# Two transformer blocks with grouped experts on one core: the uneven expert pairs in four column strips of 32

## The chip, the cores and the metric

The program runs on one core of a Trainium2 chip. The metric is the device time of one execution in microseconds (us), taken as the median of several runs; lower is better. All inputs and weights are fp32 and lie in the chip's main memory at the start. The engines are named as the profile names them: PE (TensorE, matmul), PEld (its weight loads), DVE (VectorE), ACT (ScalarE), POOL (GpSimd) and SP (SyncE, which issues the DMAs).

## What is computed

The reference chains two blocks of two layers each over 256 tokens of width 1024. The first block has feed-forward halves, an attention mixer and a gated mixer; the second has a retention and attention mixer in its first layer, a stick-breaking mixer in its second, and after each of the two a mixture of 16 experts. Only that mixture matters here:

```python
def grouped_moe(h, router_w, router_b, w_gate, w_up, w_down):
    t = h.reshape(B_ * S, D)
    scores = jax.nn.sigmoid((t @ router_w).astype(jnp.float32))
    ...            # best of four groups of experts, then the two best experts in it
    y = jnp.zeros((t.shape[0], D), jnp.float32)
    for e in range(N_EXPERTS):
        he = jax.nn.silu(t @ w_gate[e]) * (t @ w_up[e])
        y = y + combine[:, e:e + 1] * (he @ w_down[e]).astype(jnp.float32)
    return y.reshape(B_, S, D).astype(h.dtype)
```

D is 1024, an expert is 512 wide, and each token goes to two experts of one group. Which tokens go where depends on the data, so the length of each expert's list is known only while the program runs.

## The kernel before

The program is one long sequence of stages on one core. PE does nearly everything; the weights stream in through SP's queue. The last stage of each of the second block's layers is the function `moe`, called twice: once with `l=0` and once with `l=1`. I call them the first and the second expert stage.

An expert stage works on eight pairs of experts, e and e + 8, which are in different groups, so that no token is in both lists. A pair has 128 slots, and the slots lie on the columns of the stationary operand: `x[:, k, o:o+m]` holds 128 values of the width for m slots. The slots are split between the two experts at run time, in units of 32: `gi` holds 2 (64 and 64 slots), 3 (96 and 32) or 1 (32 and 96) for each pair. A pair split 64 to 64 is called even below, the others uneven. What doesn't fit comes later in a loop of extra rounds.

`products` multiplies the slots with the weights: for each k it issues a row of products whose output strips lie side by side on the 128 output partitions, `p[o:o + m, :]`, 512 columns of weights each, and the table `SEG` says which strips (first slot, how many, which expert). I call the products of one k a step. As the split is known only at run time, there are three versions of each row of products (`arm(2)`, `arm(3)`, `arm(1)`) behind two branches (L1852, L1855), and PE's sequencer jumps to the one that the pair needs. A pair has three products of eight steps: `pg` (gate), `pu` (up) and `pd` (down, in two parts of four steps, each behind branches of its own), 24 steps in all. Between `pu` and `pd` PE gathers the next pair's tokens (`ga`) and transposes (`tr`); after `pd` it brings the results back to the tokens (`py`).

The experts' weights come as pieces of 1 MB, twelve to a pair, through a ring of 20 buffers (`RING`), filled ahead while the stage before is still running. Once the ring is full, `pieces` loads in halves of 512 KB, and each load (`piece`, L1618) waits on SP until PE has finished with that half of the buffer's old contents. SP issues these in one fixed order.

Each fp32 product appears in the trace as two records (a MATMUL of PE for each, with a LDWEIGHTS of PEld), so a step of two products is four records and a step of three is six.

Of the kernel before, what the change touches and what calls it, by code (L numbers as in the profile page):

```python
# [17 lines left out]
KD = 8  # L18
T = 256
# [13 lines left out]
def _const_arrays():  # L33
    f = np.float32
    c = {}
    p = np.arange(128)
# [4 lines left out]
    t = np.arange(T)  # L41
# [27 lines left out]
    for h in range(4):  # L69
        lg = np.log(1.0 - 2.0 ** (-5.0 - h))  # L70
        for mt in range(2):
            m = (mt * 128 + p)[:, None]
# [6 lines left out]
    # the heads' means of squares from column tile ct to rows 2 ct, 2 ct + 1, and from those rows back  # L79
# [24 lines left out]
def pipeline(units, width, bg=None, rate=1):  # L104
    """advance generators side by side, oldest first; a new one joins each round while fewer than width run.
    bg: generators worked through in the background, rate steps a round"""
    units, act, bg, due = list(units), [], list(bg or []), 0
    def back(n):
        while bg and n > 0:
            if next(bg[0], bg) is bg:  # L110
                bg.pop(0)
            else:
                n -= 1
    while units or act:
        if units and len(act) < width:
            act.append(units.pop(0))
        for g in list(act):
            if next(g, act) is act:
                act.remove(g)
        due += rate  # L120
        back(int(due))
        due -= int(due)
    back(1 << 30)


def build(tc, I, out, dump=None, upto=99):
    nc = tc.nc
    coff, ctot = _const_layout()
    with ExitStack() as ctx:
# [11 lines left out]
        # the two buffers of a stage's intermediate result, in floats  # L141
# [3 lines left out]
        def big(name, shape, dt=F32):  # L145
            """the next of the 16 KB buffers for weights as they come: two for the whole program and some of the
            stage's own"""
# [6 lines left out]
        def big2(name, shape, dt=F32R):  # L154
            """the next of the 16 KB buffers for split weights"""
            return wk.tile(shape, dt, name=name, tag="whl", bufs=NW)

        def pair_of(shape, names):
            """the two 12 KB buffers that hold a stage's intermediate result in two parts"""
# [73 lines left out]
        late = []  # L233

        def spawn(gen):
            """a generator's first step now, the others a tick each: between them other products run"""
# [24 lines left out]
        def mod_out(p, b0, nt, bias, dsts):  # L261
            """p: a quarter of the columns on each quarter of the partitions, vector v on its row v"""
# [13 lines left out]
        def mod_pe(w, b0, nt, si, bias, dst, dst2=None):  # L276
            """a step for each 128 rows of w: its load, and what follows it"""
# [13 lines left out]
        def mod_first(w, b0, bias, dst, dst2, bufs, ahead_=None):  # L291
            """8 column tiles, the rows two tiles at a time, all loads at once"""
# [17 lines left out]
        def mod_dve(w, b0, nt, si, bias, dst):  # L310
            """as mod_pe"""
# [61 lines left out]
        def filler(work):  # L373
            """steps of the modulation vectors, as many as are due for the work done"""
# [13 lines left out]
        def gains(name, m, j, g, neg=False):  # L388
            """gains (1 + scale) g, or with the other sign, and shifts of chunks j + 1 and j of the modulation m"""
# [11 lines left out]
        def rsqrt(r, p, lnexp):  # L401
            """r = 1/sqrt(p + eps)"""
# [7 lines left out]
        def wsplit(src, shape):  # L410
            """the weights' upper 12 bits and the rest, exactly"""
# [10 lines left out]
        def halves(src, pin=lambda ins: ins, eng=V):  # L422
            """256 columns of weights [128, KD, 256] or [128, KD, s, t, d], as wsplit, in two steps: a function that
            gives the two parts of column tile t"""
# [27 lines left out]
        class Sum:  # L452
            """the sum of squares of the tiles given, and from it 1/sqrt(mean + eps) on every partition"""
# [14 lines left out]
            def neg_rstd(self, stat, r, pin=False):  # L468
                """-1/sqrt(mean + eps): by exp and ln, and a Newton step"""
# [20 lines left out]
        class Stream:  # L490
            """h = X G rstd + S for the matrix products: X G in two parts, S as columns 256, 257; rstd and the
            products with S come in after them (fin)"""

            def __init__(self, X, gs, tag="h", pool=None, sums=None, neg=False, u=None):
                """neg: gains and rstd of the other sign; u: X rstd, then rstd is in the products"""
# [3 lines left out]
            def shift(self):  # L499
                """S into its columns"""  # L500
# [5 lines left out]
            def start(self, late=False):  # L506
                """late: without S"""
# [16 lines left out]
            def rs(self):  # L524
                """asked for after the first products"""
# [5 lines left out]
            def product(self, name, wh, wl):  # L531
                """wh, wl: [128, KD, 128]"""
# [9 lines left out]
            def fin_act(self, dst, p, func, ps=None):  # L542
                """ps: the product with S"""
# [6 lines left out]
        def ffn(w13, w2, streams, gates, parts, gp, first=None):  # L550
            """x += half gate * (silu(h wa) * (h wb)) w2, in parts of the hidden width; first: the weights of the first
            two hidden tiles, loaded, and the steps by which the shifts come, which their products don't wait for"""
# [19 lines left out]
            def up(j0, np_, g, j):  # L572
                """g[j] = silu(h wa) (h wb)"""
# [18 lines left out]
            def early(g, j, wh, wl):  # L592
                """up, the products with the shifts after the others"""
# [37 lines left out]
            def down(j0, np_, g, d):  # L631
                """x += gate * g w2 of this part"""
# [28 lines left out]
                # the first column tile's last hidden tile comes after the second column tile's others  # L661
# [25 lines left out]
        def load13(w13, j):  # L687
            """the columns of hidden tiles j and j + 1, of both halves"""
# [6 lines left out]
        def ahead(steps, begin):  # L695
            """steps of two parts each, the first part (weights) a step ahead of the second"""
# [15 lines left out]
        def chain(items):  # L712
            """items: (raw, columns in raw, [products], consume): the weights are split an item ahead of their products;
            consume(column tile of the item, product, psum); the first step is the first weights, the others a product"""
# [15 lines left out]
            # the first product's follow-up, which asks for rstd, comes after the second product  # L730
# [24 lines left out]
        def dense(w, c0, ncols, product, consume, block=512):  # L755
            """chain items of w's columns c0..; consume(column tile, psum)"""
# [28 lines left out]
        def need(*keys):  # L785
            """the steps put off that make these"""
# [14 lines left out]
        def out_proj(raw, o, gate, early, rest, n):  # L801
            """x += gate * o w, a column tile a step; the first step is the first weights, in the next 2 n the tiles of
            `rest` are left out, to follow when they are ready; after[0](column tile): what goes on from there"""
# [54 lines left out]
        def transposes(srcs):  # L858
            """the transposes of srcs, each [128, 128], four to a bank"""
# [10 lines left out]
        def finish(d2, y=None):  # L870
            """two column tiles of the result"""
# [9 lines left out]
        # =================== first block ===================  # L881
# [5 lines left out]
        def load_x(X, src):  # L887
            """X and X rstd"""
# [16 lines left out]
        with ExitStack() as c1:  # L905
# [7 lines left out]
            # scales first, then the shifts  # L913
# [47 lines left out]
        with ExitStack() as c1:  # L961
# [7 lines left out]
            # rstd of the queries' heads: columns 4 t + 2 tt + s  # L969
# [3 lines left out]
            # a tile of queries is heads t and t + 4, so that its halves meet the two heads of the keys  # L973
# [11 lines left out]
            def head_norm(x, n, g):  # L985
                """x [128, n] in place"""
# [7 lines left out]
            def rope(x, perm, cos, sin):  # L994
                """x [128, 256] in place"""
# [25 lines left out]
            def q_in(t, p):  # L1021
                """without rstd, which comes in with the scores"""
# [15 lines left out]
            def p_in(g, p):  # L1038
                """pools: windows of 2, 4, 8, 16 tokens by doubling"""
# [34 lines left out]
            def attend(t, tt, s):  # L1074
                """head t + 4 s, queries tt"""
# [92 lines left out]
        with ExitStack() as c1:  # L1168
# [13 lines left out]
            # the second block's relative bias, its ends repeated, to DRAM  # L1182
# [72 lines left out]
        # =================== second block ===================  # L1255
# [795 lines left out]
```

## Time and profile before

| what | value |
|---|---|
| runs (us) | 2150.61, 2151.38, 2154.91 |
| median (us) | 2151.38 |
| span of the profiled execution (us) | 2151.2 |
| PE busy | 2062.4 us, 96% |
| DVE busy | 1289.6 us, 60% |
| ACT busy | 734.3 us, 34% |
| mean DMA rate over the span | 249 GB/s |
| instructions in the trace | 34307 |

The profiled execution's own time is known as its span, from the first to the last instruction; it lies 0.2 us under the median of the runs. Busy PE means that a matmul was in the array, not that the array was at its full rate: two products that run side by side on different strips count once. So the share of 96% says only that PE is hardly ever without work, and what a stretch could lose must be read from how its products follow one another.

### The profile page before, as it was taken

How to read it: one execution, taken by the hardware profiler on the slowest of the kernel's cores; microseconds unless marked ns; L12 is line 12 of the kernel's file. 1: busy time of each engine (PE TensorE's matmuls, PEld its weight loads, DVE VectorE, ACT ScalarE, POOL GpSimd, SP SyncE). 2: the span in 40 equal slices, each digit the busy share in tenths (PEclk: the TensorE clock that was granted, in tenths of full speed). 3: DMA queues.
4: the chain of work that ended last, by engine and by line, in shares of the span. 5: the costliest groups of instructions: out<-in, count | busy, mean ns of one | idle time of the engine just before them, and what ended most of it. 6: DMA issues, size and time to landing. Idle time of an engine off the chain costs nothing. (4 is left out here: it accounts for less than half of the span.)

```text
span 2151.2 us, 34307 instructions
## 1 busy us (share of the span) xinstructions
PE 2062.4 (96%) x14152; PEld 1609.6 (75%) x14152; DVE 1289.6 (60%) x2188; ACT 734.3 (34%) x1075; POOL 67.6 (3%) x60
## 2 busy tenths in 40 slices
PE   6999999999999999999999999989998998999998
PEld 5889798986799999999999998744445984222343
DVE  5367687577697888877988678532225763111122
ACT  4222132254454454356544454410003762000001
POOL 0000000020100010000100100000001000000000
PEclk8999999999999999999999999999999998999999
DMA  8678688542487686955779364799996458666793
GB/s 299 217 272 313 238 319 285 179 137 79 151 306 250 213 307 241 337 173 196 261 249 328 125 222 141 258 336 386 385 383 236 138 210 307 228 232 228 267 386 119
DMA packets 307684, 534.57 MB, mean 249 GB/s; under 512 B 12717, under 2 KB 167713, under 8 KB 294177
## 3 DMA queue, kind: packets, MB, share of 16 engines
q1 hardware_dynamic: 306960, 531.55, 70.9%
q8 instruction: 150, 2.46, 0.5%
q14 instruction: 46, 0.37, 0.0%
q10 hardware_dynamic: 528, 0.20, 0.0%
HBM read 530.64 MB, written 1.06 MB: 247 GB/s over the span
## 5 line engine op out<-in xcount | busy, mean ns | idle before, releaser
L448 PE MATMUL pa<-hh,whl 128*128 128x258 f32 (+1 forms) x880 | 252.3, 287 | 3.5 <-ACT hh L516 3.5
L449 PE MATMUL pa<-hl,whl 128*128 128x258 f32 (+1 forms) x880 | 249.3, 283 | 2.7 <-DVE hl L517 2.7
L448 PE MATMUL pb<-hh,whl 128*128 128x258 f32 (+1 forms) x880 | 249.0, 283 | 0.7 <-ACT s L564 0.7
L450 PE MATMUL pa<-hh,whl 128*128 128x258 f32 (+1 forms) x880 | 249.0, 283 | 0.0
L449 PE MATMUL pb<-hl,whl 128*128 128x258 f32 (+1 forms) x880 | 248.6, 283 | 0.0
L450 PE MATMUL pb<-hh,whl 128*128 128x258 f32 (+1 forms) x880 | 248.5, 282 | 0.0
L418 ACT ACTIVATE whl<-w13r 128x2048 fp32r<-128x2048 f32 x88 | 168.6, 1916 | 191.7 <-PE pb L450 96.0
L324 DVE SCALAR_TENSOR_TENSOR macc<-modw,cst,macc 128x1024 f32<-128x1024 f32 (+1 forms) x182 | 220.1, 1236 | 15.8 <-DMA modw<-in_w_mod_dram 14.4
L419 DVE TENSOR_TENSOR whl<-w13r,whl 128x2048 fp32r<-128x2048 f32 x88 | 201.7, 2292 | 38.0 <-ACT whl L418 37.9
L450 PE MATMUL py<-gh,whl 128*128 128x256 f32 (+1 forms) x704 | 217.0, 309 | 2.5 <-DVE whl L419 2.5
L448 PE MATMUL py<-gh,whl 128*128 128x256 f32 (+1 forms) x704 | 218.8, 311 | 0.1
L449 PE MATMUL py<-gl,whl 128*128 128x256 f32 (+1 forms) x704 | 216.8, 308 | 0.0
L448 PE MATMUL lin<-hh,whl 128*128 128x258 f32 x640 | 189.2, 296 | 5.4 <-ACT hh L516 5.4
L449 PE MATMUL lin<-hl,whl 128*128 128x258 f32 x640 | 182.5, 286 | 2.8 <-DVE hl L517 2.8
L450 PE MATMUL lin<-hh,whl 128*128 128x258 f32 x640 | 181.9, 285 | 0.0
L448 PEld LDWEIGHTS pa<-hh,whl 128*128 128x128 f32 x880 | 166.4, 189 | 11.5 <-ACT hh L516 3.7
L449 PEld LDWEIGHTS pa<-hl,whl 128*128 128x128 f32 x880 | 167.5, 190 | 3.4 <-DVE hl L517 3.1
L448 PEld LDWEIGHTS pb<-hh,whl 128*128 128x128 f32 x880 | 166.6, 189 | 1.8 <-ACT s L564 0.9
L450 PEld LDWEIGHTS pa<-hh,whl 128*128 128x128 f32 x880 | 167.1, 190 | 0.4 <-issue 0.4
L450 PEld LDWEIGHTS pb<-hh,whl 128*128 128x128 f32 x880 | 166.5, 189 | 0.4 <-issue 0.4
L449 PEld LDWEIGHTS pb<-hl,whl 128*128 128x128 f32 x880 | 166.6, 189 | 0.0
L1867 DVE TENSOR_TENSOR tm<-tm,pu 128x512 f32<-128x512 f32 x16 | 11.0, 688 | 257.0 <-PE pu L1846 257.0
(444 smaller groups left out, 3977.3 us busy)
## 6 DMA issues: line engine op xcount, KB each, us to landing
w13r<-in_ffn_w_dram SPq DMA_DIRECT2D x86, 1024.0 KB
modw<-in_w_mod_dram SPq DMA_DIRECT2D x62, 1024.0 KB
ew<-in_exp_w_down_dram SPq DMA_DIRECT2D x108, 512.0 KB
modw<-in_ada_w_dram SPq DMA_DIRECT2D x48, 1024.0 KB
ew<-in_exp_w_gate_dram SPq DMA_DIRECT2D x92, 512.0 KB
ew<-in_exp_w_up_dram SPq DMA_DIRECT2D x92, 512.0 KB
w2r<-in_ffn_w_dram SPq DMA_DIRECT2D x18, 1536.0 KB
ew<-in_exp_w_gate_dram SPq DMA_DIRECT2D x16, 1024.0 KB
```

The lines of the kernel that those rows point to most:

```text
L324: V.scalar_tensor_tensor(acc[h], x, c, acc[h], op0=OP.mult, op1=OP.add)
L418: S.activation(h, src, AF.Copy)
L419: V.tensor_sub(l, src, h.bitcast(F32))
L448: mm(p, ah, bh, start=start, stop=False)
L449: mm(p, ah, bl, start=False, stop=False)
L450: mm(p, al, bh, start=False, stop=stop)
L1867: V.tensor_mul(act, act, pu)
```

## The change

The table `SEG` is rewritten for the two uneven splits. The strip of 64 slots becomes two strips of 32 that use the same expert's weights, so an uneven step has four products of 32 columns where it had one of 64 and two of 32. The even split keeps its two strips of 64. Comments and docstrings are taken out elsewhere, which shifts line numbers by two behind this place (L1846 becomes L1848) and changes no instruction.

```diff
-                SEG = {2: ((0, 64, 0), (64, 64, 1)), 3: ((0, 64, 0), (64, 32, 0), (96, 32, 1)),
-                       1: ((0, 32, 0), (32, 32, 1), (64, 64, 1))}
+
+                SEG = {2: ((0, 64, 0), (64, 64, 1)),
+                       3: ((0, 32, 0), (32, 32, 0), (64, 32, 0), (96, 32, 1)),
+                       1: ((0, 32, 0), (32, 32, 1), (64, 32, 1), (96, 32, 1))}
```

On PE, a pair's gate product before. The names are output, moving and stationary operand: `pg` the product, `ew` the pieces of weights, `nx` the slots' tokens. The first run of rows is the version for even pairs, what follows the second branch the version for 96 to 32, and what follows the jump the version for 32 to 96:

```order
L1852 COMPARE_AND_BRANCH
L1846 MATMUL pg<-ew,nx 64x512 x16
L1852 UNCONDITIONAL_BRANCH
L1855 COMPARE_AND_BRANCH
L1846 MATMUL pg<-ew,nx 64x512
L1846 MATMUL pg<-ew,nx 32x512 x2
...
L1855 UNCONDITIONAL_BRANCH
L1846 MATMUL pg<-ew,nx 32x512 x2
L1846 MATMUL pg<-ew,nx 64x512
```

The same place after the change:

```order
L1854 COMPARE_AND_BRANCH
L1848 MATMUL pg<-ew,nx 64x512 x16
L1854 UNCONDITIONAL_BRANCH
L1857 COMPARE_AND_BRANCH
L1848 MATMUL pg<-ew,nx 32x512 x32
L1857 UNCONDITIONAL_BRANCH
L1848 MATMUL pg<-ew,nx 32x512 x32
L1857 UNCONDITIONAL_BRANCH
```

The uneven versions have 32 products of one width instead of 24 of two widths; the even version, the branches and everything around them stay where they were. The other engines' instructions stand in the same order as before.

## Rows read from the trace of the kernel before

**Rows 1.** The page: span, busy time of each engine with share and instructions.

```profile
span 2151.2 us, 34307 instructions
PE 2062.4 (96%) x14152; PEld 1609.6 (75%) x14152; DVE 1289.6 (60%) x2188; ACT 734.3 (34%) x1075; POOL 67.6 (3%) x60
```

**Rows 2.** First expert stage, two pairs: busy (records) by engine, clock, DMA, GB/s.

```profile
core 0: us, PE busy (x) PEld busy (x) DVE busy (x) ACT busy (x) POOL busy (x), PEclk, DMA share, GB/s
1419.71:1447.77 28.06, 28.04 (x156) 13.42 (x155) 6.27 (x14) 1.97 (x3) 0.00 (x0) 1.00 0.90 331
1447.77:1475.63 27.86, 27.86 (x156) 13.42 (x155) 8.01 (x18) 1.97 (x3) 0.00 (x0) 1.00 1.05 385
```

**Rows 3.** Second expert stage, same view; the last row ends the program.

```profile
1811.91:1866.70 54.79, 54.77 (x202) 14.73 (x203) 6.13 (x14) 1.97 (x3) 0.00 (x0) 1.00 0.64 220
1866.70:1921.27 54.57, 54.57 (x204) 14.72 (x203) 7.99 (x18) 1.97 (x3) 0.00 (x0) 1.00 0.67 231
...
2058.26:2086.13 27.87, 27.87 (x156) 13.41 (x155) 8.04 (x18) 1.97 (x3) 0.00 (x0) 1.00 1.05 387
...
2113.99:2151.20 37.21, 27.10 (x133) 10.89 (x132) 8.65 (x20) 4.14 (x7) 0.00 (x0) 0.95 0.09 31
```

**Rows 4.** PE by shape over the four uneven pairs: records, busy, ns.

```profile
L1846 PE MATMUL pg<-ew,nx 128*64 128x512 f32 x64 | 34.3, 618 | 0.0
...
L1846 PE MATMUL pg<-ew,nx 128*32 128x512 f32 x128 | 33.7, 604 | 0.1
```

**Rows 5.** Timeline of PE, an even pair's gate and up: start, length, records.

```profile
1419.71 7.09 PE L1846 MATMUL pg<-ew,nx 128*64 128x512 f32 x32
1426.63 7.04 PE L1846 MATMUL pu<-ew,nx 128*64 128x512 f32 x32
```

**Rows 6.** An uneven pair's gate, same view (shape of the first record).

```profile
1811.91 15.95 PE L1846 MATMUL pg<-ew,nx 128*32 128x512 f32 x48
1827.79 0.62 PE L1846 MATMUL pu<-ew,nx 128*32 128x512 f32 x2
```

**Rows 7.** One even step of line 1846: PE, PEld, clock, DMA share, GB/s.

```profile
1476.53:1477.39 0.86, 0.86 (x6) 0.29 (x4) 1.00 1.04 386
```

**Rows 8.** The same view, one uneven step.

```profile
1923.24:1925.23 1.99, 1.99 (x7) 0.34 (x6) 1.00 0.07 28
```

**Rows 9.** Line 285, four strips of 32: two steps' timeline, then one step.

```profile
89.67 1.92 PE L285 MATMUL modp<-modw,cst 128*32 128x512 f32 x16
...
90.54:91.40 0.86, 0.86 (x12) 0.13 (x4) 1.00 0.98 376
```

**Rows 10.** SP's timeline: first refills of the ring, first stage, then second.

```profile
1421.67 0.89 SPq L1618 DMA_DIRECT2D ew<-in_exp_w_down_dram  x2
...
1818.96 3.35 SPq L1618 DMA_DIRECT2D ew<-in_exp_w_down_dram  x3
```

**Rows 11.** End of the first stage: SP's last weight loads, PE's last down product.

```profile
1615.30 9.82 SPq L1618 DMA_DIRECT2D ew<-in_exp_w_down_dram  x8
...
1637.63 1.94 PE L1846 MATMUL pd<-ew,tm 128*64 128x512 f32 x8
```

**Rows 12.** Waits of PE in the whole first expert stage: total, times, longest.

```profile
PE tr L1873 <- DVE tm L1867: 0.9, 1, 0.9
PE pd L1846 <- DVE tm L1874: 0.8, 1, 0.8
```

**Rows 13.** PE's branches: count, ns min/median/max; first stage, then the uneven pairs.

```profile
L1852 PEldq COMPARE_BRANCH  x66: 63/134/3666, 1419.1 to 1636.7; - x66
...
L1852 PEldq COMPARE_BRANCH  x17: 68/207/387, 1811.1 to 2029.4; - x17
L1855 PEldq COMPARE_BRANCH  x16: 205/212/350, 1811.5 to 2014.1; - x16
```

**Rows 14.** Sequencer at the next product's branch: an uneven, an even pair.

```profile
L1852 PEldq COMPARE_BRANCH  x1: 207/207/207, 1931.2 to 1931.2; - x1
...
L1852 PEldq COMPARE_BRANCH  x2: 63/183/303, 1478.3 to 1478.6; - x2
```

## Prediction

> **What bounds the kernel now.** I read the page's first lines: PE is busy for 96% of the span [rows 1], so no other engine can be the bound for long, but a share of busy time doesn't tell whether products share the array. So I went to the stage that the change touches, pair by pair. In the first expert stage a pair takes 27.86 us, in the second the first four pairs take 54.6 to 54.8 us and the later ones 27.87 again [rows 2, 3]. The reader is to see that PE is busy from end to end in both kinds, at a granted clock of 1.00, with the same weights to read; only the time differs. By shape, the slow four are the pairs whose steps have one product of 64 columns and two of 32: 64 records of the one and 128 of the other in the gate alone, which is four pairs by eight steps [rows 4]. The first step starts with a strip of 32, so all four are split 32 to 96. All sixteen pairs of the program are in these two stages: twelve even, four uneven.
>
> Then the timeline of one gate of each kind. Even: the gate starts at 1419.71 and the up product at 1426.63, 6.92 us for eight steps [rows 5]; a step inside is 0.86 us [rows 7]. Uneven: 1811.91 to 1827.79, 15.88 us for eight steps, 1.985 us a step [rows 6, 8]. An even step has two products of 512 columns and takes 0.86 us; an uneven one has three and takes 2.3 times as long, not 1.5 times. So the strips of 64 in an even step run side by side, and in an uneven step the strip of 64 doesn't run beside the strips of 32: if the two 32s share a turn of 0.86 us and the 64 has a turn of its own, that makes 1.72 us, and 0.27 us more go at the two changes of width.
>
> **What the change removes and adds.** It acts on 4 pairs by 24 steps = 96 steps. Each loses a product of 64 columns and gets two of 32.
>
> The step after the change is in the trace already, in another stage. Line 285 multiplies four strips of 32 with 512 columns each, fp32, at clock 1.00; sixteen records, two steps, begin at 89.67 and end 1.92 us later, and the second step by itself takes 0.86 us [rows 9]. That is the even step's time to the hundredth [rows 7]. So four strips of one width share one turn. By steps: 96 x (1.985 - 0.86) = 108.0 us. The better sum goes by whole pairs, since it has the starts of the products and the work between them in it: an even pair's step takes the same 0.86 us and everything else in a pair is alike, so an uneven pair should come to an even pair's time at the same place in a stage. The first pair of a stage: 54.79 - 28.06 = 26.73 us. The others: 54.57 - 27.86 = 26.71, and twice 26.7 more. Sum 106.8 us, all of it on the path, because PE has no gap in these pairs to take it up [rows 3].
>
> What is late next: **the stream of weights.** A pair needs twelve pieces of 1,048,576 bytes; over 27.86 us that is 452 GB/s, and the first expert stage, all even, shows the engines at 385 GB/s from its second pair on [rows 2]. The ring's 20 MB head start pays the difference. That it lasts is shown there: PE waits twice in the whole stage, 0.9 and 0.8 us, both times for DVE and never for a DMA [rows 12]. The second stage after the change has the same shape, so it should get through too, but with how much to spare? In the first stage SP issues its last weight loads from 1615.30 to about 1625 [rows 11]. From the first refill at 1421.67 [rows 10] the 76 pieces behind the ring, 79.7 MB, take 207 us at 385 GB/s, to 1629; the last product that reads them starts at 1637.63 [rows 11]. Other traffic eats into that, so I put the slack at 2 to 8 us, an estimate.
>
> The change takes some of it away. A load waits until PE has told that the buffer's old contents are done with. In the first stage the first refill is issued 1.96 us after the first gate's start, behind two of eight steps; in the second, 7.05 us after it, which is three and a half uneven steps [rows 10, 2, 3, 8]. As the even version has 16 products and the uneven one 24, this fits products of the longer version being counted from its end: product 3 of 16 answers to product 11 of 24. With 32 products it would be product 19, in step 5, so the first refill comes some 5 x 0.86 + 0.25 = 4.55 us after the start (an estimate), 2.6 us later than in the first stage. With a full ring that is time lost to the engines; later in the stage the stream is behind the releases and the delay costs nothing. So 2.6 us against a slack of 2 to 8 us: nothing to 0.6 us for PE by this alone, up to 4 us if the slack is at its low end and the stream hiccups. I take 1.0 us.
>
> **The sequencer** has more to issue in less time. In an uneven pair it reached the next product's branch at 1931.2, 9.9 us or five steps after the gate's start at 1921.27: 15 of 24 products done, 9 ahead in the queue. In an even pair at 1478.3, 2.7 us or three steps after 1475.63: 6 of 16 done, 10 ahead [rows 14, 3, 2]. Nine products are 6 us of cover now and 9/4 x 0.86 = 1.9 us afterwards. A product's start costs two branches of about 0.21 us each [rows 13], so the cover holds. But a branch of the first stage took 3.67 us [rows 13], under the full DMA load that the uneven pairs will then have too, and one of those would show 3.67 + 0.4 - 1.9 = 2.2 us of idle PE. In the uneven pairs no branch took over 0.39 us. Bounds: nothing, to two such branches, 4 us. I take 1.0 us, by the first stage's rows, where long ones are rare.
>
> Everything else is unchanged: the other engines' work, the gathers, the tail of 37.21 us [rows 3], and the loop of extra rounds, which uses the even version. The code of the two uneven versions grows by a third; I price that within the branches.
>
> Sum: 2151.2 - 106.8 + 1.0 + 1.0 = 2046.4 us. The median of the runs stands 0.2 us above the profiled span; I leave that out.
>
> One thing no row shows: **three strips that stream the same weights at once.** Strips 2 to 4 of a 32-to-96 step all read the second expert's piece, while the four strips of line 285 and the two of an even step read different data. It could cost nothing or make the three take turns. I take nothing, since four different streams already run at full rate in rows 9, and one read three times is no more to deliver; the other end is a rival.
>
> **The rivals.**
>
> A, the forecast: four strips share a turn; 2046.4, from 2043 (no stall at all is 2044.4, less a little for fewer changes of width) to 2054 (both costs at their upper ends, and a little).
>
> B, the weights become the bound: if the head start is used up early, the last pairs go at the stream's pace, 12.58 MB / 385 GB/s = 32.7 us a pair instead of 27.87. Three such pairs cost 14.5 us: 2060, and four 2065. For it: 452 against 385 GB/s. Against: the first stage does exactly this without a wait [rows 12].
>
> C, the overlap is only partial. [...] Rows 9 speak against it, as in a steady row of steps the second takes 0.86 us. Worked out from rows alone: if four strips went as two turns of two, a step is 1.72 us, 96 x 0.86 = 82.6 us come back, 2129; a quarter of that, one strip in four steps late, is 2067.
>
> D, slower than before: the three strips on one piece take turns, the fourth runs beside one of them. A step is then 3 x 0.86 = 2.58 us, 96 x (2.58 - 1.985) = +57 us: 2208. It decides from 1.985 / 0.86 = 2.3 turns a step. Against it: nothing in the trace shows one stream waiting for another of different data, and one address is no harder. For it: no row has the case.
>
> **How the numbers follow.** A 0.86, B 0.05, C 0.05, D 0.04. The predicted time is A's. The range 2043 to 2054 is A's own, which I trust nineteen times in twenty, so it holds 0.82. A measurement of this kernel tells 0.2%, 4.3 us, from no change. Faster: A, B and C, 0.96. Slower: D, but a quarter of it, in which the collision stops near 2.3 turns, is no change: 0.03 and 0.01.
>
> **What would show it.** In the profile after, line 1848 should have 256 records of 32 columns in the four gates and none of 64 in these pairs; a step of eight records in 0.86 us; gate to up 6.9 us. The first four pairs of the second stage should take 28.1 and 27.9 us, with DMA at 385 GB/s from the second on, where it stood at 231 [rows 3]. A step of 1.1, 1.7 or 2.6 us would be C or D. For B, PE or PEld would wait for `ew` loads in the last pairs. The first refill should come about 4.5 us after the first gate's start; if it comes at 2 us, my reading of the releases is wrong, and if long branches show up before uneven products with PE idle behind them, the cover was too short.

## The result, and the profile after

| | before | after |
|---|---|---|
| runs (us) | 2150.61, 2151.38, 2151.68, 2154.91 | 2063.41, 2066.13, 2069.52, 2070.97 |
| median (us) | 2151.53 | 2067.82 |
| span of the profiled execution (us) | 2151.2 | 2064.4 |

The changed kernel takes 0.9603 of the time, 95% interval 0.958 to 0.9626. The forecast was 2046.4 (2043 to 2054): the sign and most of the gain came, and some 20 us of it didn't. The page's first lines [against rows 1] and its lines on the granted clock and on the queue of instruction packets (packets, MB, share of the DMA engines):

```profile
span 2064.4 us, 34691 instructions
PE 1961.0 (95%) x14344; PEld 1605.7 (78%) x14344; DVE 1289.3 (62%) x2188; ACT 734.3 (36%) x1075; POOL 67.9 (3%) x60
...
PEclk8999999999999999999999999998999999889999
...
q8 instruction: 162, 2.65, 0.5%
```

PE is busy 101.4 us less and the span is 86.8 us shorter: PE, which hardly ever waited before, now does. The same view as rows 3, pair by pair in the second expert stage (the first four pairs are the uneven ones, the last row ends the program):

```profile
core 0: us, PE busy (x) PEld busy (x) DVE busy (x) ACT busy (x) POOL busy (x), PEclk, DMA share, GB/s
1819.14:1848.19 29.05, 28.08 (x250) 13.53 (x250) 7.09 (x17) 1.98 (x3) 0.00 (x0) 1.00 0.81 292
1848.19:1876.05 27.86, 27.86 (x250) 12.79 (x250) 7.01 (x14) 1.97 (x3) 0.00 (x0) 1.00 1.05 385
...
1903.91:1937.43 33.52, 30.87 (x251) 14.26 (x250) 8.03 (x18) 1.97 (x3) 0.00 (x0) 0.95 1.04 383
...
1965.30:1994.99 29.69, 27.93 (x155) 13.42 (x155) 8.03 (x18) 1.97 (x3) 0.00 (x0) 1.00 1.03 377
1994.99:2026.83 31.84, 29.77 (x155) 14.27 (x154) 8.03 (x18) 1.97 (x3) 0.00 (x0) 0.95 1.05 386
2026.83:2064.40 37.57, 27.65 (x133) 11.46 (x132) 8.66 (x20) 4.14 (x7) 0.00 (x0) 0.89 0.32 115
```

The second pair shows what the change can do: an uneven pair in 27.86 us where it took 54.57 [rows 3], to the hundredth an even pair's time, at the DMA rate that was forecast. But others are 1 to 6 us longer, and two of those are even pairs, whose products the change doesn't touch. The first stage has only even pairs, and there, too, pairs that took 27.86 us [rows 2] are longer, at the same DMA rate:

```profile
1443.50:1471.37 27.87, 27.87 (x156) 13.43 (x155) 8.02 (x18) 1.97 (x3) 0.00 (x0) 1.00 1.05 385
...
1499.23:1530.65 31.42, 29.53 (x155) 15.06 (x154) 8.12 (x18) 1.97 (x3) 0.00 (x0) 0.95 1.05 385
```

Where the forecast without any stall, 2044.4, became 2064.4, by stretches of the two traces:

| stretch | before | after | difference |
|---|---|---|---|
| start to the first gate | 1419.71 | 1412.97 | -6.7 |
| first stage, first gate to last down product | 219.26 | 230.96 | +11.7 |
| between the stages | 172.94 | 175.21 | +2.3 |
| second stage and tail, against even pairs' times | | | +12.8 |

The first and third rows are stretches that the change doesn't touch. Part of both is the granted clock, which was at its lower level, 0.50, at other places in the two executions: ahead of the first gate for 47.8 us before and 41.0 after, between the stages for 23.9 and 30.7 (from the trace's clock records). At a clock of 0.50 the 6.8 us between the two traces are worth 3.4 at most, an estimate: half of the first row and all of the third. The rest of the first row is open; among the kernels below the same stretch takes 1412.7 to 1421.7 us, with the same code. One stretch at the lower level from each trace, of before ahead of the first stage and of after between the stages:

```profile
526.00:537.00 11.00, 11.00 (x31) 5.90 (x32) 4.76 (x14) 4.06 (x10) 0.00 (x0) 0.53 0.01 1
```

```profile
1772.50:1782.80 10.30, 10.04 (x48) 8.82 (x48) 2.88 (x9) 3.27 (x5) 0.00 (x0) 0.50 0.72 248
```

The 24.5 us of the two stages are what had to be explained. In them PE has eight waits that before's trace doesn't have, 8.0 us in the first stage and 7.4 in the second. Six are put down to "issue", that is, to nothing that the profile shows. (The waits of 0.9 and 0.8 us for DVE at the end of a stage are in both traces [rows 12].) Such a wait in PE's timeline, an even pair's gate and up and the gather behind them (start, length, records; in brackets the idle time before):

```profile
1412.97 7.09 PE L1848 MATMUL pg<-ew,nx 128*64 128x512 f32 x32
1419.89 7.04 PE L1848 MATMUL pu<-ew,nx 128*64 128x512 f32 x32
...
1429.22 2.05 PE L1817 MATMUL ga<-oh,nx 128*128 128x128 f32 x16 [2.29 <-issue]
```

Behind four of the eight the granted clock falls to 0.50 for 3.4 us, which costs some 1.7 us each, an estimate (half of the 3.4). One of them, by stretches:

```profile
1513.20:1516.50 3.30, 1.43 (x13) 1.46 (x14) 0.69 (x1) 0.00 (x0) 0.00 (x0) 1.00 1.04 382
1516.50:1519.90 3.40, 3.40 (x19) 3.40 (x18) 1.38 (x2) 0.00 (x0) 0.00 (x0) 0.50 1.04 383
1519.90:1523.30 3.40, 3.40 (x21) 1.78 (x22) 0.69 (x1) 0.00 (x0) 0.00 (x0) 1.00 1.05 389
```

Waits and clock make 15.4 + 6.8 = 22.2 of the 24.5 us. What PE waits for shows on its sequencer. The branches of line 1854 decide whether the even version runs and, behind it, jump over the two others; the profile names both kinds COMPARE_BRANCH. Their 66 executions in the first stage, and the one ahead of the stall at 1515 (duration ns, min/median/max):

```profile
L1854 PEldq COMPARE_BRANCH  x66: 63/138/6182, 1412.3 to 1641.6; - x66
...
L1854 PEldq COMPARE_BRANCH  x1: 6157/6157/6157, 1508.7 to 1508.7; - x1
```

The longest of these was 3.67 us before [rows 13]. A branch of some 6 us stands ahead of four of the eight waits. Before, five branches of PE in both stages and what follows took over 0.5 us, 15.5 us in sum; after, 23, and 71.5 us. My theory became that the code is late. The even version stands first, so an even pair's sequencer jumps over the two uneven versions, 64 products in a gate instead of 48, and **waits there for its own code**, which would come through the DMA engines like the weights. The series of even pairs that run the same products with more or less code to jump over tests that.

### The profile page after: what moved, and what is told of

The parts are those of the page before. It is cut to its first block, busy times and chain, and to the rows that moved or that the text cites. A ratio compares the mean times of both kernels' runs of the same rounds, so it can differ in the third digit from the quotient of the medians.

```text
span 2064.4 us, 34691 instructions
## 1 busy us (share of the span) xinstructions
PE 1961.0 (95%) x14344; PEld 1605.7 (78%) x14344; DVE 1289.3 (62%) x2188; ACT 734.3 (36%) x1075; POOL 67.9 (3%) x60
## 5 line engine op out<-in xcount | busy, mean ns | idle before, releaser
L418 ACT ACTIVATE whl<-w2r 128x768 fp32r<-128x768 f32 (+3 forms) x80 | 90.7, 1143 | 161.0 <-PE py L450 95.7
```

Of the source, the lines that this page charges most:

```text
L418: S.activation(h, src, AF.Copy)
```

## The experiments

All edits are against the changed kernel. The data has no pair split 96 to 32, so the entry 3 of `SEG` is code that is there and never runs.

**The code of the version that never runs, made shorter: e1_short_unused.** An even gate jumps over 40 products.

```diff
-                       3: ((0, 32, 0), (32, 32, 0), (64, 32, 0), (96, 32, 1)),
+                       3: ((0, 64, 0),),
```

> The changed kernel with the version for 96 to 32, which no pair of this data takes, cut to one strip of 64 a step (8 products instead of 32 in a gate), so its computation is left out of that version. Every pair executes the same products as in the changed kernel; only the code that an even pair jumps over shrinks, from 64 products to 40. Theory J (the lost 20 us are jumps of PE's sequencer over more code): long branches (over 0.5 us) in the two expert stages fall from 22 to 5 or fewer, the first stage's length from its first gate to its last down product goes from 231 back to about 220 us, and the time to 2044 to 2052. Theory S (four strips at a time, or the weights they pull, cost it): 2062 to 2071 as the changed kernel.

Measured: 2047.18 (2045.65 to 2051.85), ratio to before 0.9542 (0.9519 to 0.9565), as theory J said. No product that runs was changed, and the two stages are 20.9 us shorter than the changed kernel's (220.0 and 221.8 against 231.0 and 231.7, from the first gate to the last down product). The branches of the first stage, and the instruction queue:

```profile
L1854 PEldq COMPARE_BRANCH  x66: 63/132/894, 1412.0 to 1631.1; - x66
...
q8 instruction: 144, 2.36, 0.5%
```

**The old products with more code beside them: e2_grown_unused.** The uneven pairs run as before the change; the version that never runs has five strips, so an even gate jumps over 64 products as after the change.

```diff
-                       3: ((0, 32, 0), (32, 32, 0), (64, 32, 0), (96, 32, 1)),
-                       1: ((0, 32, 0), (32, 32, 1), (64, 32, 1), (96, 32, 1))}
+                       3: ((0, 32, 0), (32, 32, 0), (64, 32, 0), (96, 32, 1), (96, 32, 1)),
+                       1: ((0, 32, 0), (32, 32, 1), (64, 64, 1))}
```

> The kernel before, with its uneven pairs at 32, 32 and 64 as they were, and only the version that no pair takes grown to 40 products in a gate (a strip computed twice, so that version is not the right sum), so that an even pair jumps over 64 products as in the changed kernel. Every pair executes the very products of before. J: the even pairs of both stages stall as in the changed kernel, first stage 228 to 233 us instead of 220, the time 2160 to 2172. S or a drift between runs: 2150 to 2155, no change from before.

Measured: 2165.3 (2158.29 to 2169.99), ratio 1.0074 (1.0045 to 1.0103). Slower than before by some 16 us, under one per cent but clear of the noise, with the same products run, as theory J said. Its first stage has the changed kernel's branches and stalls, nearly to the number:

```profile
L1854 PEldq COMPARE_BRANCH  x66: 63/138/6242, 1413.8 to 1643.2; - x66
...
PE ga L1817 <- issue: 5.9, 3, 2.3
PE pu L1848 <- issue: 2.1, 1, 2.1
```

The four strips aren't needed for the loss; the code is.

**The same code without the stream of weights: e3_no_refill.** The loads that refill the ring are left out, so that later products read old weights; `KEPT` is empty.

```diff
+                        if again and n % 12 not in KEPT:
+                            for j, t in enumerate(todo[n:n + 2]):
+                                wpiece[t] = rows4(bufs[(n + j) % RING])
+                            continue
```

> The changed kernel without the loads behind the ring's first 20 pieces: the later pairs multiply whatever the buffers hold, so the result is not the reference's; PE's products, branches and code are the same. It tells whether a jump is slow because the instructions come over the same engines as the weights. J with contention: long branches stay as many but shrink from 2 to 6 us to under 2 us, PE's stalls behind them go, and the time is 2040 to 2048. J without contention (the fetch itself is the price): long branches of 2 to 6 us stay, time 2058 to 2068.

The time missed its expectation: 2095.99 (one run). Other results of the first stage send tokens to other experts, and the loop of extra rounds runs at the end, 42.4 us by itself. The stages show what was asked. The branches of the first stage, the second stage, and the extra round:

```profile
L1859 PEldq COMPARE_BRANCH  x66: 63/133/1319, 1418.2 to 1635.7; - x66
...
1813.13:2032.87 219.74, 218.09 (x1474) 103.17 (x1474) 60.69 (x129) 15.11 (x23) 0.00 (x0) 1.00 0.01 3
2042.03:2084.42 42.39, 32.60 (x146) 15.55 (x146) 5.73 (x12) 1.28 (x2) 0.00 (x0) 0.94 0.82 300
```

The code has the changed kernel's size and comes in the same 162 packets, but no branch takes over 1.32 us and both stages take 219 to 220 us. The long branches didn't stay as many, as I had expected with contention: there are 7. So it isn't the jump alone: with the weights' 385 GB/s beside the code the longest branch of the first stage took 6.18 us, with the 3 GB/s here 1.32. The code is late where it is fetched beside the weights.

**The version that never runs as two products: e4_wide_unused.** An even gate jumps over 48 products, as before the change.

```diff
-                       3: ((0, 32, 0), (32, 32, 0), (64, 32, 0), (96, 32, 1)),
+                       3: ((0, 96, 0), (96, 32, 1)),
```

> A version that could stand: the changed kernel with the version for 96 to 32 as a strip of 96 and one of 32 (16 products in a gate), so an even pair jumps over 48 products, as many as before the change. No pair of this data takes that version. J: long branches as before the change (4 in the expert stages), time 2044 to 2054. S: 2062 to 2071. If the size of the jump matters in steps, not in proportion, it lies with the kernel before and not between.

Measured: 2043.2 (2040.48 to 2044.9), ratio 0.9514 (0.9493 to 0.9534), the fastest of all, 0.8 us under the lower end of J. An uneven and an even pair of the second stage, and the branches of the first:

```profile
1893.13:1920.99 27.86, 27.86 (x252) 12.77 (x251) 8.04 (x18) 1.97 (x3) 0.00 (x0) 1.00 1.05 385
...
1976.71:2004.57 27.86, 27.86 (x155) 13.42 (x155) 8.03 (x18) 1.97 (x3) 0.00 (x0) 1.00 1.04 384
...
L1854 PEldq COMPARE_BRANCH  x66: 63/132/3612, 1416.6 to 1634.2; - x66
```

This is the prediction's sum without stalls, 2044.4. What a pair split 96 to 32 would take in this version isn't known, since none runs.

**The even version last: e5_even_last.**

```diff
-                        with tc.If(gr_ == 2) as c:
-                            arm(2)
+                        with tc.If(gr_ == 1) as c:
+                            arm(1)
...
-                                arm(1)
+                                arm(2)
```

> The changed kernel with its three versions in another order: 32 to 96 first, then 96 to 32, then even. The code has the same length (80 products in a gate), but an even pair now jumps twice over 32 products ahead of its products and falls through behind them, instead of once over 64 behind them. If the length of one jump decides (J1): the even pairs' long branches go, time 2044 to 2054. If the length of the code that has to come in decides, wherever the jumps stand (J2): 12 or more long branches stay, time 2060 to 2070.

Measured: 2086.36 (2081.8 to 2089.33), ratio 0.9696 (0.9675 to 0.9717), slower than the changed kernel and above both expectations. The long branches are as many as after the change (23), four of them of 5.8 to 5.9 us, and the stalls have moved to the products behind them (first stage):

```profile
PE pg L1848 <- issue: 5.5, 3, 3.4
PE pu L1848 <- issue: 4.8, 2, 2.9
```

The order doesn't take the waits for code away. That it makes them dearer fits the jump now standing ahead of the products, with less in flight to cover it; this is argued, not shown.

**Between 48 and 64: e6_three_strips_96.** 56 products to jump over.

```diff
-                       3: ((0, 32, 0), (32, 32, 0), (64, 32, 0), (96, 32, 1)),
+                       3: ((0, 64, 0), (64, 32, 0), (96, 32, 1)),
```

> Half of the change: only the version for 32 to 96, which this data takes, has four strips; 96 to 32 keeps 64, 32, 32. An even pair jumps over 24 + 32 = 56 products, between the 48 of before and the 64 of the change. If stalls grow with the jump: half of the change's extra long branches, first stage about 225 us, time 2050 to 2060. If there is a step between 48 and 64: either 2042 to 2048 or 2063 to 2070.

Measured: 2046.8 (2045.31 to 2048.58), ratio 0.952 (0.9502 to 0.9538): the step, not the proportion. Long branches do become more, 14, but the longest takes 3.72 us, and in the first stage PE doesn't wait behind them. What it does wait for there is DVE, 1.6 us ahead of a transpose; in the second stage one wait of 0.8 us ends as the waits for code do, 1.4 us after a block has landed.

```profile
L1854 PEldq COMPARE_BRANCH  x66: 72/140/3722, 1414.1 to 1633.2; - x66
```

**88 products to jump over: e7_grown_twice.** The old uneven version 32 to 96 runs; the one that never runs has eight strips.

```diff
-                       3: ((0, 32, 0), (32, 32, 0), (64, 32, 0), (96, 32, 1)),
-                       1: ((0, 32, 0), (32, 32, 1), (64, 32, 1), (96, 32, 1))}
+                       3: ((0, 32, 0), (32, 32, 0), (64, 32, 0), (96, 32, 1)) * 2,
+                       1: ((0, 32, 0), (32, 32, 1), (64, 64, 1))}
```

> As the run with the kernel before's products and a grown version that is not taken, with 64 products in it (each strip computed twice, so that version's sum is wrong): an even pair jumps over 64 + 24 = 88 products. If the stalls grow with the jump, the first stage takes 235 to 245 us and the time is 2170 to 2185; if they have a ceiling, 2160 to 2170 as with 64.

Measured: 2209.13 (one run), 58 us over before with the same products run, and above both expectations: the loss goes on growing with the jump. 38 long branches, 151 us in sum. The instruction packets and the others in its first stage, which takes 252 us:

```profile
q1 hardware_dynamic: 43520, 81.80, 89.2%
q8 instruction: 43, 0.70, 1.2%
```

**The small code with the even version last: e8_wide_even_last.** The edits of e4 and e5 together.

> The best so far (96 to 32 as a strip of 96 and one of 32) with the even version last: an even pair jumps over 32 and over 16 products ahead of its own. J1: no long branches in even pairs, 2040 to 2046, the same as with the even version first or up to 3 us less; J2: the same 2 to 4 long branches, no difference.

Measured: 2048.38 (2044.43 to 2048.66), ratio 0.952 (0.9501 to 0.954), above the expected 2046 and not clearly apart from e4. Eleven long branches, in the first stage none over 2.8 us, one wait of 0.9 us there and one of 2.4 us in the second stage:

```profile
PE pg L1848 <- issue: 2.4, 1, 2.4
```

So the order costs much only together with the larger code.

**What of the code decides: e9_half_jumps and e10_gate_long_up_short.** Two readings were left: the amount of code that comes by in a time, or the length of a single jump. e9 keeps the amount and halves the jumps; e10 keeps e6's amount in a gate and up together, but jumps over 72 products in the gate, which reads its strips from `SEGG`, and over 40 in the up, which reads them from `SEGU`.

```diff
-                    products(pg, xg_b, KD, lambda k: (w_("exp_w_gate_2", k // 4), k % 4), gr_)
-                    products(pu, xg_b, KD, lambda k: (w_("exp_w_up_2", k // 4), k % 4), gr_)
+                    for ks in (range(0, 4), range(4, 8)):
+                        products(pg, xg_b, KD, lambda k: (w_("exp_w_gate_2", k // 4), k % 4), gr_, ks)
+                    for ks in (range(0, 4), range(4, 8)):
+                        products(pu, xg_b, KD, lambda k: (w_("exp_w_up_2", k // 4), k % 4), gr_, ks)
```

> The changed kernel, with the gate and the up product each put behind branches of their own in two halves of four steps. The products that run, their order and the 80 products of code to each of the rows gate, up and down stay; an even pair now jumps twice over 32 products in a gate and not once over 64. It is to say what makes the even pairs wait: the length of one jump, or the amount of code that comes by in a time. Theory R (rate): the code of all versions streams through in order, 256 bytes a product, in blocks of 16 KB of which one starts at most every 5.9 to 6.0 us while the weights load (smallest distances of instruction packets in the traces of before and after). A gate's 80 products are 20 KB, 7.4 us of fetching, against the 6.93 us that an even gate runs. Halving the jumps changes none of this, so the time stays near the changed kernel's 2067.8: 2060 to 2075, with stalls of PE of about 2 us and branches up to some 6 us. Theory L (length): a jump over 48 or 56 products (12 or 14 KB) is covered and one over 64 (16 KB, a whole block) isn't; with jumps of 32 all are covered, and the time falls to 2043 to 2050, with no branch over 4 us.

Measured: 2069.1 (2067.07 to 2070.64), ratio 0.9626 (0.96 to 0.9652). By its time theory R; by its rows not. PE's waits and branches in the first stage:

```profile
PE py L1897 <- DVE dd L1890: 5.5, 4, 1.9
...
PE pg L1848 <- issue: 0.3, 1, 0.3
...
L1854 PEldq COMPARE_BRANCH  x98: 63/134/3722, 1412.1 to 1640.0; - x98
```

The waits named "issue" have shrunk from 8.0 to 0.3 us in the first stage, and no branch there takes over 3.72 us (4.05 in the whole run), near to what theory L said. In the second stage the waits that end just behind a block of code make 0.7 us against 7.4. The time went elsewhere: with the rows cut in two, the work was put in another order, in some pairs gate and up alternate by halves, and in others `py` waits for DVE, 5.5 us in either stage; the mean granted clock of the execution is 0.978, against 0.982 in e6. In the first stage the last block had landed 3.3 to 5.6 us before each of the long ones ended, so by that sign they aren't waits for code. Another wait of 2.1 us, in the second stage, ends 5.6 us after a landing; the sequencer loads registers there (L1922). So its time tells nothing of the code, and its rows speak for L, as far as a run with another order of the work can.

```diff
-                       3: ((0, 32, 0), (32, 32, 0), (64, 32, 0), (96, 32, 1)),
+                       3: ((0, 64, 0), (64, 32, 0), (96, 32, 1)),
...
+                SEGG = {**SEG, 3: ((0, 32, 0), (32, 32, 0), (64, 32, 0), (96, 32, 1), (96, 32, 1))}
+                SEGU = {**SEG, 3: ((0, 64, 0),)}
```

> The code of e6_three_strips_96 distributed in another way: the 96-to-32 version, which this data never takes, has five strips a step in the gate, one in the up product and three in the down product, where e6 had three in all. What runs is as in the changed kernel. An even pair's gate jumps over 72 products (18 KB, more than a block), its up product over 40; a gate and an up together hold 144 products of code as in e6, where one of 56 is jumped over in each. Theory R (rate): 144 products are 36 KB, 13.4 us of fetching at 5.95 us a block, against 13.9 us that an even pair's gate and up run; the gate alone (88 products, 22 KB, 8.2 us) is 1.25 us over its 6.93 us, which the ten or so products in flight cover. The time stays by e6's 2046.8: 2043 to 2051, with 156 instruction packets. Theory L (length): a jump over more than a block isn't covered, so the twelve even gates wait as the changed kernel's rows do, and half or more of its 24 us come: 2054 to 2062, with branches of some 6 us at the gates.

Measured: 2053.57 (2050.97 to 2056.18), ratio 0.955 (0.9523 to 0.9578), between the two: above R's 2051 and under L's 2054. In the first stage no even gate costs anything, against L (first line below). In the second the stage is 7.5 us longer than in e6 (228.2 against 220.7 us): 3.0 us of waits in two uneven pairs and an even one and, against R, one even gate with a branch of the long kind. That branch, and the wait behind it, as the profile names it, follow:

```profile
L1856 PEldq COMPARE_BRANCH  x66: 63/138/3702, 1414.6 to 1634.8; - x66
...
L1856 PEldq COMPARE_BRANCH  x1: 6234/6234/6234, 1928.5 to 1928.5; - x1
...
PE pu L1850 <- DMA ew<-in_exp_w_gate_dram: 2.1, 1, 2.1
```

It is put down to a load of weights, but PE starts at 1935.05, 0.3 us after the branch ends at 1934.75, and not with a weight load's landing; a wait with a DMA's name can be one for code. The two runs together say that neither the amount nor the length alone sets the cost.

**The series.** First stage, from the first gate to the last down product, with its longest branch; long branches are those over 0.5 us from there to the end of the program:

| kernel | jumped in a gate | instruction packets | longest branch of the first stage, us | long branches | first stage, us | time, us |
|---|---|---|---|---|---|---|
| e1 | 40 | 144 | 0.89 | 2 | 220.0 | 2047.18 |
| before | 48 | 150 | 3.67 | 5 | 219.3 | 2151.53 |
| e4 | 48 | 150 | 3.61 | 7 | 219.3 | 2043.2 |
| e6 | 56 | 156 | 3.72 | 14 | 220.8 | 2046.8 |
| after | 64 | 162 | 6.18 | 23 | 231.0 | 2067.82 |
| e2 | 64 | 162 | 6.24 | 19 | 231.0 | 2165.3 |
| e7 | 88 | 180 | 6.54 | 38 | 251.8 | 2209.13 |
| e3, no weights | 64 | 162 | 1.32 | 7 | 219.2 | |

Each step of eight products in the jump adds exactly six packets. A packet is 16,384 bytes by its record (I call it a block of code), and the program has 16 pairs by 3 rows of products: 6 x 16,384 / (48 x 8) = 256 bytes a product. So **the code of versions that don't run was fetched all the same.** The packets' times, worked out from their records, tell when. Under the weights' load of the first stage two packets start 5.8 to 5.9 us apart at the closest, but for one distance each after the change, in e2 and in e9, three in e5 and nine of 42 in e7; 13 of the changed kernel's 33 distances there lie within 5.7 to 6.2 us, 4 of before's 27. Without weights (e3) they come as close as 3.0 us. And every long branch of every kernel, from 0.5 to 6.8 us, ends 1.3 to 1.6 us after a packet has landed. The eight waits of the changed kernel, each with the block that landed last before PE went on:

```
block starts   lands      PE goes on at   idle before it, us   the profile names
1425.94        1426.94    1429.22  ga     2.29                 issue
1512.41        1513.53    1515.07  ga     1.89                 issue
1599.70        1600.80    1602.08  ga     1.75                 issue
1622.27        1623.39    1625.06  pu     2.04                 issue
1845.69        1846.74    1848.19  pg     0.95                 PE py
1913.27        1914.36    1915.65  pu     2.65                 issue
1978.64        1979.73    1981.01  ga     1.76                 issue
2001.34        2002.47    2004.14  pu     2.06                 a load of ew
```

PE goes on 1.3 to 2.3 us after a landing each time, and two of the eight carry another name in the profile. The waits are of two kinds. Those at 1429, 1515, 1625 and 2004 stand behind a branch of 6.0 to 6.2 us, which ends 0.2 to 0.8 us before PE goes on. Ahead of the other four no branch took over 0.4 us: the sequencer had passed it and, by the landings, ran out of code in the straight run behind it, at 1915.65 in the midst of an uneven pair's up product. The branch ahead of the wait at 1602.08:

```profile
L1854 PEldq COMPARE_BRANCH  x1: 384/384/384, 1595.9 to 1595.9; - x1
```

So, by this sign, it wasn't only jumps that ran out of code: PE went on at 1602.08, 1.3 us after a landing. In e7 the code is the pace: 43 packets in 252 us are one every 5.86 us.

By the number of blocks in the first stage, beside 385 GB/s of weights: with 25 to 31 PE waits for code in no kernel, but for 0.9 us in e8; with 34 or 43, e9 apart, it waits for 8.0 us (after) and more (e7).

**What stays open:** when a block is asked for. In before, e4, e6, e9 and e10 the longest branch of the first stage takes 3.6 to 3.7 us, which the work in flight mostly covers (ten products ahead, by estimate 4.3 us in an even pair [rows 14, 7]). Branches of some 6 us come only where an even pair jumps over 64 products, 16 KB, or more, in one jump or, in e5, in two of 32 one right behind the other; but not each such jump pays, as e10 shows. In all 13 branches of 5.8 to 6.3 us of after, e2, e5 and e10 the block that ends them starts 3.3 to 3.8 us after the branch begins and 6.3 to 11.7 us after the block before it. So the closest distance of 5.9 us is not what held them; it fits a block that is asked for only at the branch, but no record shows the asking. Which gates pay may hang on where the borders of the blocks fall in the code, which each edit shifts: after and e2, with 80 products to a gate in the same order, have their first stage's four waits at the same four places, to 0.1 us. No run moved the borders alone.

## Right or wrong, step by step

**The gain: right.** A step of four strips takes an even step's time. In the first uneven pair the up follows the gate after 6.87 us (6.9 forecast), 0.86 us a step, and three strips on one piece cost nothing, so C and D fall. The undisturbed uneven pairs take 27.86 us; the 106.8 us came in full, as e4 shows at 2043.2 against 2044.4. That C's 2067, by a step of 1.1 us (0.86 and a quarter more), lies by the measured 2067.82 is a coincidence: no step is slow, and the time went elsewhere.

```profile
1819.14 7.07 PE L1848 MATMUL pg<-ew,nx 128*32 128x512 f32 x64
1826.01 7.08 PE L1848 MATMUL pu<-ew,nx 128*32 128x512 f32 x64
```

**The weights: right in the mechanism, and cheap.** The first refill in the second stage was forecast 4.55 us after the gate's start; it came 4.54 after it:

```profile
1823.68 2.69 SPq L1618 DMA_DIRECT2D ew<-in_exp_w_down_dram  x5
```

The loss of head start that I priced at 1.0 us can't be told from the rest after the change, and e4, at 2043.2, shows none clear of the noise. B is refuted: in the second stage of e4 and e6 PE waits for no load, and in that of e1 for 0.4 us.

**The sequencer: wrong, and this is the whole miss.** e4 runs the changed kernel's products with less unused code and takes 24.6 us less by the medians, 19 by the ratios to before (0.9514 and 0.9603). Two sentences of the prediction failed. "The code of the two uneven versions grows by a third; I price that within the branches": I priced the branches at the uneven pairs' entries, where the cover shrinks to 1.9 us, and took 1.0 us with a bound of 4. The price of the code is paid in even pairs as well, which hold six of the eight waits. After the change it was 15.4 us of waits and, by estimate, 6.8 us of clock behind them, 22.2 of the 24.5 us by which the two stages are longer; no run shows what the other 2.3 are. I had written that the even version stays where it was; its products do, and the code around them doesn't.

The second is the bound, "two such branches, 4 us". The branch of 3.67 us was in my rows [rows 13], and I counted it as a rare event of a given size. It was the sign of a wait near the end of its cover: 3.7 us behind ten products that last 4.3. What would have warned was in the same trace, in a queue that I hadn't read: 28 instruction packets in the first stage, and the closest 5.92 us apart beside the weights, while a gate runs 6.92 us on one block of code (64 products by 256 bytes). With 80 products it is a block and a quarter, by that distance 7.4 us of fetching, an estimate. This is a warning and not a sum: e10's gates hold 88 products and cross the first stage without a wait for code.

**The range:** its upper end had 4 us for the branches and nothing more for the code. The chances for B, C and D, all on PE's work or the weights, missed the one mechanism that came.

## To carry to other kernels

Where a choice is made by branches, look at the size of every version, also of one that never runs: here it was fetched all the same (162 packets with 64 products to jump over, 150 with 48) and delayed what ran beside it (e2, 1.0074 of before's time with the same products run). Before versions are unrolled further, read the queue of instruction packets and the longest branches in the trace; a branch of some microseconds that costs nothing yet is a warning: here it took 3.67 us, and beside 385 GB/s of weights its cover was gone with 4 KB more of code to a gate. Two wide products a step for the split that this data doesn't have gave all of it back (0.9514 against 0.9603); what they cost where that split comes wasn't measured.

## What the runs showed of the hardware that I had not expected

- Code that is jumped over was fetched, six packets of 16 KB for eight more products in each of 48 rows, through the whole series from 144 to 180. By the landings PE ran out of code in a straight run as well as at a branch: four of the eight waits stand behind no branch of over 0.4 us and end 1.3 to 1.5 us after a landing.
- Beside 385 GB/s of weights two 16 KB blocks of code seldom started closer together than 5.9 us (5.92 at the closest before; 5.78, but for one of 3.23, after); without the weights they came as close as 3.0 us (e3). A packet itself took 1.1 us beside 370 GB/s or more and 1.0 to 1.1 us beside less than 50 (medians of before and after).
- A stall of 1.9 us in an otherwise busy PE was followed by 3.4 us at a granted clock of 0.50, so that this wait cost nearly twice its length (an estimate). It happened behind four of the eight; behind another of 2.29 us the clock stayed at 1.00.
- Strips of one width shared a turn also where three of them read the same weights: 0.86 us a step (6.87 us for the eight steps of an uneven gate).
